# Pooling's differences and the low parts of weights moved between the values, and a queue of loads in program order

## The chip, the cores and the metric

The kernel runs on one core of a Trainium2 chip. The metric is the time of one execution in device microseconds (us); with more cores it would be that of the slowest. The engines are named as in the profile: PE is TensorE (matmuls; PEld its loads of weights), DVE is VectorE, ACT is ScalarE, POOL is GpSimd, and SP is SyncE, which in this kernel only issues DMAs. SP issues its DMAs one after another, and a DMA that has to wait for its data holds back those behind it in the queue.

## The reference, cut to what matters

One block of a transformer with two branches, for one sequence of 1024 positions, a width of 1024 and 16 heads, in float32:

```python
mod = silu(c) @ w_ada + b_ada
shift, scale, gate = split(mod, 3)
h = rms_norm(x, norm_gain) * (1 + scale) + shift
q, k, v, z_a, u, z_b, m_a, m_b = split(h @ w_in, 8)     # each 1024 columns

attn = stick_breaking_attention(q, k, v)                # strictly causal
p_a = (attn * silu(z_a)) @ w_branch_a

# four groups of 256 channels, windows 2, 4, 8, 16
d = trailing_mean(u, window of the group) - u
pooled = (d @ pool_w[group]) * pool_scale
p_b = (pooled * silu(z_b)) @ w_branch_b

merged = sigmoid(m_a) * p_a + sigmoid(m_b) * p_b
return rms_norm(x + gate * (merged @ w_out), final_gain)
```

The change is in how and when d, the parts of the weights in w_in, and the inputs of w_branch_b are prepared. What is computed stays the same.

## The kernel before

**Products.** TensorE multiplies in a rounded form of float32 (`F32R`). To keep the accuracy, each operand is split in a high part (a rounded copy) and a low part (the operand minus its high part), and a product takes three matmuls for each block of 128 rows: high times high, high times low, low times high (`mm3`, lines 152 to 160). A weight tile is 128x1024 (512 KB): eight blocks of 128x128. A tile gives two outputs of 128x512 ("halves" of the sequence), each of 8 x 3 = 24 matmuls, so a tile has 48 matmuls. `split` (lines 103 to 108) makes the two parts, on the engines that its caller names: the high part is a copy (line 116 on VectorE, line 112 on ScalarE), the low part a subtraction (line 107). `load_w` (lines 118 to 121) loads a weight tile on SP's queue and splits it; the raw tiles (tag "raw") and the split ones (tag "whl") have two buffers each.

**Stages in program order.** The input is normed and modulated and turned into h (kept in on-chip memory as high and low part), and the columns of u are computed and stored to DRAM (`u_d`). Then follow four stages that the change touches:

- *The values* (lines 346 to 366): v is computed in 2 x 8 outputs (half of the columns hf, block of positions sb) and stored to `v_d`.
- *The pooling* (lines 370 to 418): for each of four groups (window win), two differences d of 128 channels each are made from u_d on VectorE: the load of u, log2(win) additions for the window sum (line 386), the subtraction (line 390), the tail (lines 392, 393), and the split (lines 116, 107 into dhl). Then for each of the group's two outputs j: a tile of the z_b product (`project`, weights wzb, high part on VectorE, low part on GpSimd), its silu into zs (lines 403, 404), the pool product (two outputs of 6 matmuls, with the small weights phl), the scale (line 416), and the split into gb (lines 417, 418).
- *The product with w_branch_b* (lines 421 to 435): for each of eight tiles j, the weights wb_j are loaded and split (high part on VectorE, low part on GpSimd), a tile wg_j of w_gate is loaded and added up into gacc (VectorE, lines 427, 429), and two outputs pb are computed, copied by ScalarE to sm (line 433) and stored to DRAM by SP (line 434).
- *The gate*, then attention, in which the remaining products of w_in run.

**Low parts made early.** The products during attention use 40 tiles of w_in. For the first 8 (`PLAIN`) the low part is made when they are used. For the other 32 (numbers 8 to 39) it is made ahead by `make_lo` (lines 131 to 140): SP loads the tile (l_raw), ScalarE copies the high part (l_hi), VectorE subtracts it in place, and SP stores the result to `wl_d`. One each is made with the second halves of u (8), then with each output of the values as `LO_V` says (7 in each half hf, 14 in all), and with each tile of the product with w_branch_b as `LO_PB` says (10).

**What sets the order.** A scheduler orders each engine's instructions. It may move an instruction ahead of others of its engine that are not bound to it. An instruction that is given to `tc.keep_in_program_order` is placed behind the instruction that was traced before it on the same engine. Before the change that is used for the first stages only (`pinned`, and `load` at line 204). From the values on, SP's loads are ordered by the scheduler. Tiles come from pools; where a pool is closed, later pools may use its memory.

## Time and profile before

| | us |
|---|---|
| median of 3 runs | 1263.06 |
| range of the 3 runs | 1262.25 to 1266.24 |
| the profiled execution | 1256.96 |
| its span (first to last instruction) | 1255.2 |

The profile is that of one execution. A row of instructions in a timeline gives the start (us from the span's start), the duration, the engine, the line of the kernel, the operation, out<-in by the program's names, the sizes, and in brackets the time that the engine stood idle before it and what it waited for. "SPq" is SP's queue as it issues a DMA. A row by line gives out<-in and the count of instructions, then busy time, mean ns of one, and the idle time just before them with what ended it. A row of DMAs ends with the median us from issue to landing. The granted clock is the share of full speed that the throttle allowed TensorE. In time, the stages that the change touches stand at 125 to 212 us (the values), 212 to 331 (the pooling) and 331 to 419 (the product with w_branch_b).

### The profile page before, as it was taken

The page shows a single profiled execution, that of the slowest core. Times are in us where ns is not written, and L with a number is a line of the kernel's source. Part 1 is how long each engine was busy: PE and PEld are TensorE (multiplying, and loading weights), DVE is VectorE, ACT ScalarE, POOL GpSimd, SP SyncE. Part 2 cuts the span into 40 slices and gives each one's busy share as a digit, 9 for nine tenths or more (in the row PEclk, how much of TensorE's full clock was granted, in tenths as well). Part 3 has the DMA queues.
Part 4 walks back from the last instruction along what each step waited for, and adds up shares of the span by engine and source line. Part 5 has one row for each costly group of instructions (what it writes and reads, how often), then busy time and mean ns, then how long its engine had stood idle before and what let it go on. Part 6 is the DMA issues. An engine that isn't in the chain of part 4 may idle for free.

```text
span 1255.2 us, 16268 instructions
## 1 busy us (share of the span) xinstructions
PE 1225.7 (98%) x5838; PEld 1015.9 (81%) x5838; DVE 808.5 (64%) x1092; ACT 548.9 (44%) x1029; POOL 223.9 (18%) x373
## 2 busy tenths in 40 slices
PE   7999999899999999999999999999999999899997
PEld 6888888678888888888888888888888888788886
DVE  6624442999511168786887878788786864675653
ACT  5554331321110256565556656566665654331101
POOL 1100010111212333322322222122222310000001
PEclk9999999999999999999999999999999999999999
DMA  9539995862344411133323333232233237964522
GB/s 358 212 135 341 321 360 166 293 203 93 116 143 134 160 42 55 65 125 102 106 78 95 117 101 126 90 107 70 92 123 101 92 107 227 374 215 147 192 64 84
DMA packets 72803, 192.46 MB, mean 153 GB/s; under 512 B 7697, under 2 KB 21009, under 8 KB 70802
## 3 DMA queue, kind: packets, MB, share of 16 engines
q1 hardware_dynamic: 61954, 172.28, 40.1%
q10 hardware_dynamic: 10768, 19.14, 4.6%
q8 instruction: 46, 0.75, 0.2%
q14 instruction: 35, 0.29, 0.1%
HBM read 136.86 MB, written 50.34 MB: 149 GB/s over the span
## 4 chain that ended last, share of the span: by engine, by line
PE 77%; issue 9%; DVE 6%; DMA 3%; POOL 2%; ACT 1%; SPq 0%; POOLq 0%; DVEq 0%; ACTq 0%
PE p L92 24%; PE pb L92 7%; PE v L92 7%; PE pa L92 7%; PE o L92 6%; PE wzb L92 5%; PE u L92 4%; PE z L92 4%; PE av L92 4%; PE wt L92 4%; PE ua L92 3%; DVE om L574 1%; PE pool L92 1%; DVE be L575 1%; DMA l_raw<-in_w_in 1%
## 5 line engine op out<-in xcount | busy, mean ns | idle before, releaser
L92 PE MATMUL p<-hT,w 128*128 128x512 f32 x1920 | 534.5, 399 | 0.0
L92 PEld LDWEIGHTS p<-hT,w 128*128 128x128 f32 x1920 | 341.5, 188 | 56.6 <-issue 0.5
L574 DVE TENSOR_TENSOR_SCAN om<-om 128x512 f32<-128x512 f32 (+7 forms) x128 | 175.2, 1368 | 52.3 <-POOL om L572 28.8
L567 ACT ACTIVATE om<-z 128x512 f32<-128x512 f32 (+2 forms) x192 | 94.5, 492 | 103.8 <-PE z L92 101.4
L594 DVE TENSOR_TENSOR wt<-wt,wt 128x512 fp32r<-128x512 f32 (+1 forms) x160 | 100.9, 631 | 46.6 <-ACT wt L593 45.2
L572 POOL TENSOR_SCALAR_AFFINE_SELECT om<-om 128x128 f32<-128x128 f32 x128 | 65.0, 508 | 328.3 <-ACT om L567 302.6
L593 ACT CAST wt<-wt 128x512 fp32r<-128x512 f32 (+1 forms) x160 | 87.3, 546 | 68.6 <-PE wt L92 64.9
L575 DVE TENSOR_TENSOR be<-be,om 128x511 f32<-128x511 f32 (+7 forms) x128 | 99.7, 779 | 10.8 <-DVE om L574 0.5
L92 PE MATMUL pa<-ga,wa 128*128 128x512 f32 x384 | 92.1, 397 | 3.5 <-ACT m_sg L178 3.5
L92 PE MATMUL av<-wt,vv 128*128 128x512 f32 x320 | 94.4, 376 | 0.0
L92 PEld LDWEIGHTS wt<-ident,be 128*128 128x128 f32 x576 | 72.1, 140 | 27.5 <-DVE wt L594 3.2
L568 ACT ACTIVATE be<-z 128x512 f32<-128x512 f32 (+2 forms) x192 | 93.5, 487 | 0.0
L92 PE MATMUL wt<-ident,be 128*128 128x128 f32 x576 | 89.2, 273 | 3.8 <-DVE wt L594 3.8
L92 PE MATMUL wzb<-hT,wzb 128*128 128x512 f32 x384 | 92.3, 396 | 0.0
L92 PE MATMUL o<-wo,mhl 128*128 128x512 f32 (+1 forms) x408 | 89.8, 377 | 0.0
L92 PEld LDWEIGHTS pa<-ga,wa 128*128 128x128 f32 x384 | 73.2, 191 | 20.3 <-ACT m_sg L178 3.9
L92 PE MATMUL pb<-gb,wb 128*128 128x512 f32 x384 | 88.1, 391 | 0.0
L92 PE MATMUL v<-wv,hT 128*128 128x512 f32 x384 | 87.2, 389 | 0.0
L92 PEld LDWEIGHTS wzb<-hT,wzb 128*128 128x128 f32 x384 | 73.1, 191 | 16.3 <-DVE zs L404 0.3
L92 PEld LDWEIGHTS o<-wo,mhl 128*128 128x128 f32 x408 | 73.5, 188 | 14.4
L92 PEld LDWEIGHTS pb<-gb,wb 128*128 128x128 f32 x384 | 72.1, 188 | 15.8
L92 PEld LDWEIGHTS v<-wv,hT 128*128 128x128 f32 x384 | 72.1, 188 | 15.0
(119 smaller groups left out, 1482.9 us busy)
## 6 DMA issues: line engine op xcount, KB each, us to landing
w_raw<-in_w_in SPq DMA_DIRECT2D x40, 512.0 KB, 4.5
l_raw<-in_w_in SPq DMA_DIRECT2D x32, 512.0 KB, 5.6
wl_d<-l_raw SPq DMA_DIRECT2D x32, 512.0 KB, 5.1
w<-wl_d SPq DMA_DIRECT2D x32, 512.0 KB, 3.8
v_d<-vo SPq DMA_DIRECT2D x16, 512.0 KB, 5.2
vv<-v_d SPq DMA_DIRECT2D x8, 1024.0 KB, 5.7
wa_raw<-in_w_branch_a SPq DMA_DIRECT2D x16, 512.0 KB, 4.6
wa<-in_w_mod SPq DMA_DIRECT2D x7, 1024.0 KB, 9.0
```

The lines of the kernel that those rows point to most:

```text
L92: ins = op(*args, **kw)
L567: act.activation(om[:, b0:b0 + n], zp[:, :n], AF.Sigmoid, scale=-0.125)
L568: act.activation(be[:, b0:b0 + n], zp[:, :n], AF.Sigmoid, scale=0.125)
L572: gp.affine_select(out=tl[:, :P], in_=tl[:, :P], pattern=[[1, P]], compare_op=ALU.is_gt, fill=fill, base=0, channel_multiplier=-1)
L574: v.tensor_tensor_scan(om[:, :W], om[:, :W], om[:, :W], 1.0, ALU.mult, ALU.min)
L575: v.tensor_mul(be[:, 1:W], be[:, 1:W], om[:, :W - 1])
L593: act.copy(wt[:, 0, :off], pt[:, :off])
L594: v.tensor_sub(wt[:, 1, :off], pt[:, :off], wt[:, 0, :off].bitcast(F32))
```

## The change

It has four parts.

1. *Differences.* They leave the pooling's loop and become a function, `make_d(j)`. Three are called during the values (`DIFFS`: behind outputs 1, 5 and 10), the other five during the pooling, behind the z_b product of outputs 0, 2, 3, 4 and 5 (`DIFFS_POOL`). They have a pool of their own ("dif") and dhl has four buffers instead of three.
2. *Low parts of w_in.* The values make 3 in each half instead of 7 (6 instead of 14), the pooling makes 10 (`LO_POOL`, none before), the product with w_branch_b makes 8, one a tile (`LO_PB`, 10 before). `make_lo` has two raw buffers instead of three and makes each tile in two halves of 128x512 with one small buffer for l_hi.
3. *The z_b product* splits its weights on ScalarE (high part) and VectorE (low part) instead of VectorE and GpSimd.
4. *The queue.* `issue_paced` issues a DMA on SP and, from the start of the values to the end of the product with w_branch_b, keeps it in program order. It is used by `load_w`, by the load of make_lo, by the load of u and by the store of the values. The store of make_lo, the loads of praw and wg, and the stores of sm are issued as before.

Beside these, zs (and sm) has two buffers instead of three, gacc and bg have memory of their own, and the pool "first" lies on the other side of memory.

```diff
 PLAIN = 8
-LO_V = (1, 1, 1, 1, 1, 1, 1, 0)
-LO_PB = (1, 1, 1, 1, 1, 1, 2, 2)
+LO_V = (0, 1, 0, 1, 0, 1, 0, 0)
+LO_PB = (1, 1, 1, 1, 1, 1, 1, 1)
+
+DIFFS = {1: 0, 5: 1, 10: 2}
+
+DIFFS_POOL = {0: 3, 2: 4, 3: 5, 4: 6, 5: 7}
+LO_POOL = (1, 1, 1, 1, 1, 1, 2, 2)
...
+    paced = [False]
+
+    def issue_paced(dst, src):
+        ins = nc.sync.dma_start(dst, src)
+        if paced[0]:
+            tc.keep_in_program_order(ins)
+
     def load_w(src, name, hi_eng, lo_eng):
         raw = wts.tile([P, KB, P], F32, tag="raw", bufs=2, name=name + "_raw")
-        nc.sync.dma_start(raw.rearrange("p k c -> p (k c)"), src)
+        issue_paced(raw.rearrange("p k c -> p (k c)"), src)
         return split(raw, [P, KB, P], wts, "whl", 2, hi_eng, lo_eng, name)
...
         for _ in range(n):
             i = next(early_lo)
-            raw = pl.tile([P, D], F32, tag="lraw", bufs=3, name=f"l{i}_raw")
-            nc.sync.dma_start(raw, a["w_in"][tiles[i]])
-            hi = pl.tile([P, D], F32R, tag="lhi", bufs=1, name=f"l{i}_hi")
-            act.copy(hi, raw)
-            v.tensor_sub(raw.bitcast(F32R), raw, hi.bitcast(F32))
+            raw = pl.tile([P, D], F32, tag="lraw", bufs=2, name=f"l{i}_raw")
+            issue_paced(raw, a["w_in"][tiles[i]])
+            for hf in range(2):
+                part = raw[:, hf * 512:hf * 512 + 512]
+                hi = pl.tile([P, 512], F32R, tag="lhi", bufs=1, name=f"l{i}_hi{hf}")
+                act.copy(hi, part)
+                v.tensor_sub(part.bitcast(F32R), part, hi.bitcast(F32))
             nc.sync.dma_start(wl_d[i], raw)
 
     def load_parts(i, name):
...
     early = ExitStack()
-    first = early.enter_context(pool("first"))
+    first = early.enter_context(pool("first", side="right"))
...
+    invn = const.tile([P, 16], F32, name="invn")
+    for j in range(16):
+        gp.memset(invn[:, j:j + 1], 1.0 / (16 - j))
+    dhls = {}
+
+    def make_d(j):
+        win = WINDOWS[j // 2]
+        u = dif.tile([P, S + 16], F32, tag="u", bufs=2, name=f"u{j}")
+        v.memset(u[:, S:], 0.0)
+        issue_paced(u[:, :S], u_d[j])
+        cur, n, step = u, S + 16, 1
+        while step < win:
+            nxt = dif.tile([P, S + 16], F32, tag="win", bufs=2, name=f"win{j}_{step}")
+            n -= step
+            v.tensor_add(nxt[:, :n], cur[:, :n], cur[:, step:step + n])
+            cur, step = nxt, 2 * step
+        t0 = S - win + 1
+        d = dif.tile([P, S], F32, tag="win", bufs=2, name=f"d{j}")
+        v.scalar_tensor_tensor(d[:, :t0], cur[:, :t0], 1.0 / win, u[:, :t0], ALU.mult, ALU.subtract)
+        tl = dif.tile([P, 16], F32, tag="tl", bufs=2, name=f"tl{j}")
+        v.tensor_mul(tl[:, :win - 1], cur[:, t0:S], invn[:, 16 - win + 1:])
+        v.tensor_sub(d[:, t0:], tl[:, :win - 1], u[:, t0:S])
+        dhls[j] = split(d, [P, S], dif, "dhl", 4, v, v, f"dhl{j}")
+
+
+    lows = ExitStack()
+    lo = lows.enter_context(pool("lo"))
     with pool("vp") as vp:
...
             use[i](1, ps)
-            make_lo(vp, 1)
+            make_lo(lo, 1)
+        early.close()
+        diffs = ExitStack()
+        dif = diffs.enter_context(pool("dif", side="right"))
+        paced[0] = True
...
                 v.tensor_sub(vo[:, :, 1], pv, vo[:, :, 0].bitcast(F32))
-                nc.sync.dma_start(
+                issue_paced(
                     v_d[4 * hf:4 * hf + 4, :, sb].rearrange("n p c -> p n c"),
                     vo.rearrange("p (n h) i d -> p n (h i d)", h=2).bitcast(F32),
                 )
-                make_lo(vp, LO_V[sb])
-    early.close()
-
-
-    with pool("pb") as pb:
-        invn = pb.tile([P, 16], F32, name="invn")
-        for j in range(16):
-            gp.memset(invn[:, j:j + 1], 1.0 / (16 - j))
+                make_lo(lo, LO_V[sb])
+                if 8 * hf + sb in DIFFS:
+                    make_d(DIFFS[8 * hf + sb])
+
+
+    with ExitStack() as ctx_pb:
+        pb = ctx_pb.enter_context(pool("pb"))
         gb = pb.tile([P, 2, KB, S], F32R, name="gb")
         for g, win in enumerate(WINDOWS):
-            dhl = []
-            for cb in range(2):
-                j = 2 * g + cb
-                u = pb.tile([P, S + 16], F32, tag="u", bufs=2, name=f"u{j}")
...
-                dhl.append(split(d, [P, S], pb, "dhl", 3, v, v, f"dhl{j}"))
+            dhl = [dhls[2 * g], dhls[2 * g + 1]]
             praw = wts.tile([P, 2, 256], F32, tag="raw", bufs=2, name=f"praw{g}")
             nc.sync.dma_start(praw, a["pool_w"][g].rearrange("(k p) d -> p k d", p=P))
             ph, pl_ = split(praw, [P, 2, 256], pb, "phl", 1, v, v, f"phl{g}")
             for ob in range(2):
                 j = 2 * g + ob
-                zs = [pb.tile([P, 512], F32, tag="zs", bufs=3, name=f"zs{j}_{sh}") for sh in range(2)]
+                zs = [pb.tile([P, 512], F32, tag="zs", bufs=2, name=f"zs{j}_{sh}") for sh in range(2)]
 
                 def silu(sh, ps):
                     act.activation(zs[sh], ps, AF.Sigmoid)
                     v.tensor_mul(zs[sh], ps, zs[sh])
 
-                project(CZB + j, f"wzb{j}", silu, v, gp)
+                project(CZB + j, f"wzb{j}", silu, act, v)
+                if j in DIFFS_POOL:
+                    make_d(DIFFS_POOL[j])
                 for sh in range(2):
                     sl = slice(sh * 512, sh * 512 + 512)
                     ps = bank("tr", f"pool{j}_{sh}")
...
                     v.scalar_tensor_tensor(z, ps, psc_v[:, j:j + 1], z, ALU.mult, ALU.mult)
                     act.copy(gb[:, 0, j, sl], z)
                     v.tensor_sub(gb[:, 1, j, sl], z, gb[:, 0, j, sl].bitcast(F32))
-        gacc, bg = (pb.tile([P, S + 16], F32, tag="u", bufs=2, name=n)[:, :D] for n in ("gacc", "bg"))
+                make_lo(lo, LO_POOL[j])
+        diffs.close()
+        late = ctx_pb.enter_context(pool("late", side="right"))
+        gacc, bg = (late.tile([P, D], F32, name=n) for n in ("gacc", "bg"))
         nc.sync.dma_start(bg, a["b_gate"].broadcast_to([P, D]))
         for j in range(KB):
-            sm = [pb.tile([P, 512], F32, tag="zs", bufs=3, name=f"sm{j}_{sh}") for sh in range(2)]
+            sm = [pb.tile([P, 512], F32, tag="zs", bufs=2, name=f"sm{j}_{sh}") for sh in range(2)]
             whl = load_w(a["w_branch_b"][j], f"wb{j}", v, gp)
             wg = wts.tile([P, D], F32, tag="raw", bufs=2, name=f"wg{j}")
             nc.sync.dma_start(wg, a["w_gate"][j * P:(j + 1) * P, :])
...
                 mm3(ps, whl, (gb[:, 0], gb[:, 1]), range(KB), hmov(sh))
                 act.copy(sm[sh], ps)
                 nc.sync.dma_start(pb_d[j][:, sh * 512:sh * 512 + 512], sm[sh])
-            make_lo(pb, LO_PB[j])
+            make_lo(lo, LO_PB[j])
 
         for hf in range(2):
             sl = slice(hf * 512, hf * 512 + 512)
...
         nc.sync.dma_start(g_d, bg[0:1, :])
+    lows.close()
+    paced[0] = False
```

How the change moves instructions is shown at three places. The rows are one engine's instructions in their order, each with its line, operation, out<-in and size; the lines before and after the change differ by some numbers.

The first place is SP's queue from the end of the pooling into the first tiles of the product with w_branch_b. wb1_raw is the second weight tile of that product, wg a tile of w_gate, sm the copied results, sm0_0 those of the first half of tile 0, l32_raw a tile of w_in whose low part is made, wl_d its store. Before:

```order
L120 DMA wb1_raw_2507<-in_w_branch_b 128x1024
L425 DMA wg1_2512<-in_w_gate 128x1024
L120 DMA wb2_raw_2577<-in_w_branch_b 128x1024
L425 DMA wg2_2582<-in_w_gate 128x1024
L120 DMA wb3_raw_2647<-in_w_branch_b 128x1024
L434 DMA pb_d_74<-sm0_0_2435 128x512
L434 DMA pb_d_74<-sm0_1_2436 128x512
L425 DMA wg3_2652<-in_w_gate 128x1024
L434 DMA pb_d_74<-sm1_0_2505 128x512
L120 DMA wb4_raw_2717<-in_w_branch_b 128x1024
```

After:

```order
L457 DMA wg0_2536<-in_w_gate 128x1024
L466 DMA pb_d_74<-sm0_0_2529 128x512
L466 DMA pb_d_74<-sm0_1_2530 128x512
L127 DMA l32_raw_2593<-in_w_in 128x1024
L155 DMA wl_d_76<-l32_raw_2593 128x1024
L127 DMA wb1_raw_2604<-in_w_branch_b 128x1024
L457 DMA wg1_2609<-in_w_gate 128x1024
L466 DMA pb_d_74<-sm1_0_2602 128x512
L466 DMA pb_d_74<-sm1_1_2603 128x512
L127 DMA l33_raw_2666<-in_w_in 128x1024
L155 DMA wl_d_76<-l33_raw_2666 128x1024
```

Before, the load of wb3 stands ahead of the stores of tile 0, and that of wb4 ahead of the second store of tile 1. After, the load of wb1 stands behind both stores of tile 0, the load of l32 and the store of its low part, and the next tile repeats this.

The second place is VectorE's order where the values end and the pooling begins. vo7_1 is the last output of the values, phl0 the small weights of the first group, dhl0 the split difference of the first 128 channels, zs0_0 the first silu. Before:

```order
L361 TENSOR_TENSOR vo7_1_1609<-v7_1_1584,vo7_1_1609 128x8x64
L380 MEMSET u0_1636 128x16
L380 MEMSET u1_1649 128x16
L116 CAST phl0_1664<-praw0_1662 128x512
L107 TENSOR_TENSOR phl0_1664<-praw0_1662,phl0_1664 128x512
L404 TENSOR_TENSOR zs0_0_1667<-wzb0_0_1674,zs0_0_1667 128x512
L386 TENSOR_TENSOR win0_1_1639<-u0_1636 128x1039
L390 SCALAR_TENSOR_TENSOR d0_1641<-win0_1_1639,u0_1636 128x1023
L392 TENSOR_TENSOR tl0_1643<-win0_1_1639,invn_1618 128x1
L393 TENSOR_TENSOR d0_1641<-tl0_1643,u0_1636 128x1
L386 TENSOR_TENSOR win1_1_1652<-u1_1649 128x1039
L116 CAST dhl0_1646<-d0_1641 128x1024
```

After:

```order
L407 TENSOR_TENSOR vo7_1_1668<-v7_1_1643,vo7_1_1668 128x8x64
L154 TENSOR_TENSOR l22_raw_1778<-l22_raw_1778,l22_hi0_1780 128x512
L154 TENSOR_TENSOR l22_raw_1778<-l22_raw_1778,l22_hi1_1783 128x512
L121 CAST phl0_1679<-praw0_1677 128x512
L112 TENSOR_TENSOR phl0_1679<-praw0_1677,phl0_1679 128x512
L431 TENSOR_TENSOR zs0_0_1682<-wzb0_0_1689,zs0_0_1682 128x512
L112 TENSOR_TENSOR wzb1_1791<-wzb1_raw_1789,wzb1_1791 128x1024
L154 TENSOR_TENSOR l23_raw_1868<-l23_raw_1868,l23_hi0_1870 128x512
L431 TENSOR_TENSOR zs0_1_1683<-wzb0_1_1716,zs0_1_1683 128x512
L445 SCALAR_TENSOR_TENSOR zs0_0_1682<-pool0_0_1758,vecs_86,zs0_0_1682 128x512
L154 TENSOR_TENSOR l23_raw_1868<-l23_raw_1868,l23_hi1_1873 128x512
L445 SCALAR_TENSOR_TENSOR zs0_1_1683<-pool0_1_1768,vecs_86,zs0_1_1683 128x512
```

Before, the window sums, the subtractions and the splits of the first differences follow phl0. After, they are gone from here, since the first differences stand among the values; the low parts of w_in (l22, l23) and of the second z_b weights (wzb1) stand in their place.

The third place is VectorE's order where the pooling ends and the product with w_branch_b begins. wb0 and wb1 are the first two weight tiles of that product, gb the split results of the pooling, zs7 the last output's silu and scale. Before:

```order
L416 SCALAR_TENSOR_TENSOR zs6_0_2270<-pool6_0_2331,vecs_86,zs6_0_2270 128x512
L416 SCALAR_TENSOR_TENSOR zs6_1_2271<-pool6_1_2341,vecs_86,zs6_1_2271 128x512
L429 SCALAR_TENSOR_TENSOR gacc_2432<-wg1_2512,csilu_97,gacc_2432 128x1024
L418 TENSOR_TENSOR gb_1635<-zs6_0_2270,gb_1635 128x512
L418 TENSOR_TENSOR gb_1635<-zs6_1_2271,gb_1635 128x512
L404 TENSOR_TENSOR zs7_0_2351<-wzb7_0_2358,zs7_0_2351 128x512
L116 CAST wb1_2509<-wb1_raw_2507 128x1024
L404 TENSOR_TENSOR zs7_1_2352<-wzb7_1_2385,zs7_1_2352 128x512
L416 SCALAR_TENSOR_TENSOR zs7_0_2351<-pool7_0_2412,vecs_86,zs7_0_2351 128x512
L416 SCALAR_TENSOR_TENSOR zs7_1_2352<-pool7_1_2422,vecs_86,zs7_1_2352 128x512
L418 TENSOR_TENSOR gb_1635<-zs7_0_2351,gb_1635 128x512
L418 TENSOR_TENSOR gb_1635<-zs7_1_2352,gb_1635 128x512
```

After:

```order
L431 TENSOR_TENSOR zs7_0_2423<-wzb7_0_2430,zs7_0_2423 128x512
L431 TENSOR_TENSOR zs7_1_2424<-wzb7_1_2457,zs7_1_2424 128x512
L445 SCALAR_TENSOR_TENSOR zs7_0_2423<-pool7_0_2484,vecs_86,zs7_0_2423 128x512
L445 SCALAR_TENSOR_TENSOR zs7_1_2424<-pool7_1_2494,vecs_86,zs7_1_2424 128x512
L447 TENSOR_TENSOR gb_1676<-zs7_0_2423,gb_1676 128x512
L447 TENSOR_TENSOR gb_1676<-zs7_1_2424,gb_1676 128x512
L121 CAST wb0_2533<-wb0_raw_2531 128x1024
L459 TENSOR_SCALAR gacc_2526<-wg0_2536,csilu_97 128x1024
L154 TENSOR_TENSOR l32_raw_2593<-l32_raw_2593,l32_hi0_2595 128x512
L154 TENSOR_TENSOR l32_raw_2593<-l32_raw_2593,l32_hi1_2598 128x512
L121 CAST wb1_2606<-wb1_raw_2604 128x1024
L461 SCALAR_TENSOR_TENSOR gacc_2526<-wg1_2609,csilu_97,gacc_2526 128x1024
```

Before, the high part of wb0 is made ahead of these rows and that of wb1 ahead of the last scale. After, the high part of wb0 follows the pooling's last results, and that of wb1 follows the low part of l32.

14 lines of the change are left out of this document (removed).

## The prediction

> **What bounds the kernel now.** I read the page's busy shares first, then busy time by stage, then the chain of waits of TensorE, then the timeline of the stage that the change touches.
>
> ```profile
> span 1255.2 us, 16268 instructions
> PE 1225.7 (98%) x5838; PEld 1015.9 (81%) x5838; DVE 808.5 (64%) x1092; ACT 548.9 (44%) x1029; POOL 223.9 (18%) x373
> ```
>
> TensorE is busy for 98% of the span, so any change can gain little, and anything that makes TensorE wait is paid in full. The next rows are busy times by stage (start and end, length, PE, PEld, DVE, ACT, POOL, granted clock, DMA share, GB/s): the values, the pooling with its z_b product, and the product with w_branch_b.
>
> ```profile
> 125.00:212.00 87.00, 87.00 (x385) 72.05 (x384) 32.92 (x34) 26.81 (x33) 5.27 (x18) 1.00 0.82 289
> 212.00:331.40 119.40, 112.21 (x482) 90.94 (x481) 109.08 (x142) 29.00 (x42) 21.29 (x8) 0.99 0.54 185
> 331.40:419.30 87.90, 87.90 (x386) 72.12 (x385) 13.91 (x15) 10.61 (x18) 17.56 (x8) 1.00 0.38 129
> ...
> PE pool L92 <- DVE phl L116: 4.0, 1, 4.0
> PE pool L92 <- DVE u L380: 3.1, 1, 3.1
> ...
> 254.00:256.00 2.00, 2.00 (x6) 1.61 (x5) 2.00 (x3) 0.92 (x1) 0.00 (x0) 0.50 0.39 160
> 256.00:258.00 2.00, 2.00 (x7) 1.56 (x7) 2.00 (x4) 0.12 (x1) 0.00 (x0) 0.68 0.58 59
> ```
>
> In the values TensorE never waits and VectorE works 33 us of 87. In the pooling VectorE works 109 us of 119, and TensorE waits for it twice, 4.0 and 3.1 us. After the longer wait the granted clock was 0.50 for 2 us and 0.68 for 2 us: 1.0 + 0.64 = 1.6 us more. That is all there is to gain here: 7.1 + 1.6 = **8.7 us**. In the product with w_branch_b TensorE never waits. Why, the timeline shows:
>
> ```profile
> 331.38 88.06 PE L92 MATMUL pb<-gb,wb 128*128 128x512 f32 x384
> ...
> 342.57 0.59 ACT L433 COPY sm<-pb 128x512 f32<-128x512 f32 x1 [3.94 <-PE pb L92]
> 342.62 0.69 DVE L116 CAST wb<-wb_raw 128x1024 fp32r<-128x1024 f32 x1 [5.60 <-PE pb L92]
> 343.18 0.33 SPq L434 DMA_DIRECT2D pb_d<-sm  x1
> 343.40 2.41 POOL L107 TENSOR_TENSOR wb<-wb_raw,wb 128x1024 fp32r<-128x1024 f32 x1 [11.32 <-DVE wb L116]
> 345.83 0.33 SPq L425 DMA_DIRECT2D wg<-in_w_gate  x1
> 348.06 0.59 ACT L433 COPY sm<-pb 128x512 f32<-128x512 f32 x1 [4.91 <-PE pb L92]
> 348.67 0.32 SPq L434 DMA_DIRECT2D pb_d<-sm  x1
> 349.43 1.28 DVE L429 SCALAR_TENSOR_TENSOR gacc<-wg,csilu,gacc 128x1024 f32<-128x1024 f32 x1 [6.12 <-DMA wg<-in_w_gate]
> 350.75 0.33 SPq L120 DMA_DIRECT2D wb_raw<-in_w_branch_b  x1
> 353.60 0.59 ACT L433 COPY sm<-pb 128x512 f32<-128x512 f32 x1 [4.95 <-PE pb L92]
> ...
> 419.52 0.59 ACT L433 COPY sm<-pb 128x512 f32<-128x512 f32 x1 [4.91 <-PE pb L92]
> ```
>
> A weight tile lasts 353.60 - 342.57 = 11.03 us. The load at 350.75 is that of a tile two ahead; the cast at 342.62 waited for a buffer that TensorE had just left, not for data. Weights are ready a whole tile early.
>
> **The change, part by part.**
>
> *Pooling (gain).* The order puts differences 0 to 3 between the values, so at the start of pooling only phl stands ahead of the first pool product. Four differences cost VectorE 21 us (two of 4.65 and two of 5.9, by the rows below: window sum, subtraction, cast, low part). In the values it then works about 33 + 21 us, less the l tiles that leave, of 87: hidden. In the pooling it loses 21 us, gains 8 low parts of wzb at 1.2 and loses 8 casts at 0.69: about 92 of 112. I take both waits as gone: **-8.7 us**. If the cover fails, up to 7 us stay.
>
> ```profile
> L386 DVE TENSOR_TENSOR win<-u 128x1039 f32<-128x1039 f32 x8 | 9.9, 1234 | 0.3 <-DMA u<-u_d 0.3
> L390 DVE SCALAR_TENSOR_TENSOR d<-win,u 128x1023 f32<-128x1023 f32 x2 | 2.4, 1216 | 0.0
> L417 ACT CAST gb<-zs 128x512 fp32r<-128x512 f32 x16 | 9.9, 621 | 36.0 <-DVE zs L416 32.0 <-DVE u L380 3.9
> L418 DVE TENSOR_TENSOR gb<-zs,gb 128x512 fp32r<-128x512 f32 x16 | 10.8, 680 | 0.1
> L416 DVE SCALAR_TENSOR_TENSOR zs<-pool,vecs,zs 128x512 f32<-128x512 f32 x16 | 11.6, 742 | 2.3 <-PE pool L92 2.2
> ...
> l_raw<-in_w_in SPq DMA_DIRECT2D x32, 512.0 KB, 5.6
> ...
> wb_raw<-in_w_branch_b SPq DMA_DIRECT2D x8, 512.0 KB, 3.4
> ...
> 164.61 0.32 SPq L140 DMA_DIRECT2D wl_d<-l_raw  x1
> 165.03 0.38 SPq L136 DMA_DIRECT2D l_raw<-in_w_in  x1
> ```
>
> *Product with w_branch_b (loss).* Here the order of SP's queue changes. The load of l is pinned behind the two stores of the tile's result, the load of the next wb behind wl_d, the store of l's low part. SP issues one row after the other, and each of these waits for its data. So from the end E of a tile's last matmul everything follows in series, where before it lay a tile ahead:
>
> - copy of the last half 0.08 after E (331.38 + 88.06 = 419.44; copy 419.52); its store 0.61 after the copy's start (348.67 - 348.06); next issue 0.42 later (164.61 to 165.03): load of l at E + 1.11
> - landing as for wb alone, 3.4: E + 4.5
> - two halves, each a cast on ScalarE (0.62) and a low part on VectorE (0.68); the one lhi buffer keeps them in series: 2.6, with hand-overs 2.7: E + 7.2
> - wl_d, then wb 0.42 later: E + 7.65
> - wb's landing: no trace row has this pair alone. Bounds: 3.4 (wb alone) and 5.6 (l among others). I take 4.4, near the alone row, as one 512 KB store runs just ahead: E + 12.0
> - cast 0.69, hand-over 0.09, low part on GpSimd 2.41: E + 15.2. Four matmuls need only the high part and run meanwhile.
> - 44 matmuls at 88.06/384 = 0.229, and 0.16 until the last has drained (0.39 long, 0.23 apart): E + 25.5
>
> A tile takes 25.5 us instead of 11.03: **+14.4 us**. TensorE has stood still some 12 us each time, so the clock will fall as it did at 254. That costs between nothing and 1.6 us, as the four early matmuls and the wait for GpSimd may absorb it; I take 1.0. Tiles 1 to 7: 7 x 15.4 = **+108 us**.
>
> The Trainium skill ("TensorE: Matmul & The Clock Gate", Part 1: The HAM clock gate) says that TensorE falls to half rate after an idle window of about 3.4 us and needs about as long in work to recover. The rows at 254 and 256 agree. By it every restart would cost an estimated 1.7 us, and the total would be 5 us higher.
>
> *First tile of that product.* Before, wb0 was cast while pooling still ran. Now its cast stands behind pooling's last results on VectorE: scale 0.74, cast 0.62, low part 0.68, cast of wb0 0.69, low part 2.41, hand-overs 0.3 = 5.4 us after the last pool product, less four matmuls, 0.9: **+4.5 us**. Between 0, if wb0's row can be served earlier, and 7 with a cold clock.
>
> *At nothing:* smaller lhi (the l casts are hidden where TensorE has other tiles: ScalarE is 44% busy), two zs buffers instead of three, memory sides, invn moved to the start. In the pooling, each odd wzb load is also pinned behind a wl_d. From the start of a tile it takes about 4 us to the load, 3.4 to 5.6 to land, 1.05 + 1.2 for its parts: at most 12, against 48 x 0.229 + 12 x 0.24 = 13.9 us. It fits, with 2 us to spare in the worst case. The loads of u wait for nothing late. In the values v_d's stores stand behind l's, but have three buffers. After the product, the first K and Q tiles load unpinned, and attention is as before.
>
> Sum: 108 + 4.5 - 8.7 = **+104 us**. The profiled execution took 1256.96 us (span 1255.2), the median of the three runs 1263.06, 0.5% more. On the median: 1263 + 104 = **1367 us**.
>
> **The rivals.**
>
> 1. *Not slower: the loads stay ahead.* If l's load and the next wb's were issued at a tile's start, their chain (3.4 + 2.7 + 4.4 + 3.2 = 14 us) could mostly lie beside its 11 us, and with loads a tile further ahead, as the load at 350.75 is, entirely. Then only pooling's gain is left: 1263 - 9 = 1254. It decides itself at one point: whether SP reaches wb's row before the store of the tile under way has its data. For it: the buffers would allow it. Against: the order has store, store, l, wl_d, wb. 3%.
> 2. *Longer: GpSimd is held by VectorE.* In the trace two VectorE operations lasted 3.11 and 3.44 instead of 1.2 while GpSimd formed a low part:
>
> ```profile
> 225.78 2.40 POOL L107 TENSOR_TENSOR wzb<-wzb_raw,wzb 128x1024 fp32r<-128x1024 f32 x1 [35.75 <-DVE wzb L116]
> 226.16 3.11 DVE L107 TENSOR_TENSOR dhl<-d,dhl 128x1024 fp32r<-128x1024 f32 x1
> 239.17 3.44 DVE L390 SCALAR_TENSOR_TENSOR d<-win,u 128x1021 f32<-128x1021 f32 x1
> ```
>
> So the later of two waits for the earlier. gacc (1.28) now follows wb's cast at once if wg has landed by then; if it starts in the 0.09 us before GpSimd does, each tile grows by 1.2: +8.4, 1375. Against it: wg is issued 0.42 behind wb, behind two other transfers. 14%. The Trainium skill ("SBUF — State Buffer", SBUF: two separate sides) says that a VectorE operation with two SBUF inputs and a GpSimd one lock each other out for a whole instruction; the two rows agree.
> 3. *Longer: pooling waits for wzb too.* VectorE's rows now hold wzb's low parts behind differences. If four odd tiles came 5 us late: +20, 1387. 10%.
> 4. *Shorter: half the chain is hidden,* because l's tile is served before TensorE ends: 7 us a tile less, 1318. 5%.
>
> **How the numbers follow.** Forecast 68%, rivals 3, 14, 10 and 5%. Low end: wb at 3.4, no clock loss, no first-tile loss: 7 x 13.4 - 9 = 85, 1348. High end: both landings at 5.6 (+3.4 a tile), clock at 1.6 (+0.6), the lock (+1.2): 7 x 20.6 - 4 = 140, 1403. Range **1346 to 1402**; it leaves out rivals 1 and 4 and corners. A measurement here can tell about 0.3% from no change: faster 3%, the same 1%, slower 96%.
>
> **What would show it.** In the changed profile: TensorE waiting for DVE wb seven times, about 12 us each, in a stage of some 200 us instead of 88; SP rows in the order store, store, l, wl_d, wb; granted clock near half at each restart; no wait of pool for phl or u. Wrong would be: wb's load issued before the store of its tile, tiles of 11 us, or waits of that size in pooling.

## The result and the profile after

| | before | changed |
|---|---|---|
| median | 1263.35 us (4 runs, 1262.25 to 1266.24) | 1376.55 us (4 runs, 1375.46 to 1377.45) |
| profiled execution, its span | 1256.96, 1255.2 us | 1375.46, 1373.4 us |
| ratio to before | | 1.0915, 95% interval 1.0888 to 1.0941 |

The changed kernel is 9.15% slower. The first rows are from its page.

```profile
span 1373.4 us, 16307 instructions
PE 1244.6 (91%) x5838; PEld 1026.3 (75%) x5838; DVE 821.2 (60%) x1124; ACT 561.9 (41%) x1069; POOL 203.0 (15%) x365
```

TensorE's share fell from 98% to 91%. Busy time by stage, with the columns of the prediction's table (start and end, length, PE, PEld, DVE, ACT, POOL, granted clock, DMA share, GB/s), shows where:

```profile
125.00:216.30 91.30, 88.89 (x386) 73.15 (x385) 43.49 (x66) 21.47 (x35) 0.00 (x0) 0.98 0.66 218
216.30:325.30 109.00, 109.00 (x481) 89.82 (x479) 84.03 (x119) 38.59 (x60) 0.00 (x0) 1.00 0.53 181
325.30:539.40 214.10, 111.85 (x389) 83.70 (x390) 40.15 (x35) 19.18 (x32) 21.56 (x9) 0.74 0.28 95
```

The third stage is the product with w_branch_b, with the four gate matmuls that end it. The same stage before:

```profile
331.40:420.60 89.20, 89.20 (x390) 72.70 (x388) 14.18 (x16) 11.69 (x20) 17.56 (x8) 1.00 0.38 127
```

So the values took 91.3 us instead of 87.0 (+4.3), pooling 109.0 instead of 119.4 (-10.4), the product 214.1 instead of 89.2 (+124.9). What follows, 834.0 us (1373.4 - 539.4), was 834.6 before (1255.2 - 420.6). These make +118.2, the difference of the two spans. What TensorE waited for in the changed kernel's stages (total, times, longest):

```profile
PE pb L97 <- DVE wb L121: 97.6, 8, 13.8
...
PE pb L97 <- POOL wb L112: 3.2, 7, 1.3
PE v L97 <- DVE vo L407: 2.4, 1, 2.4
...
PE gate L97 <- DVE gacc L461: 1.4, 1, 1.4
```

The waits of pool for phl and u are gone. In their place stand eight waits for wb. One of them from end to end, in the timeline of the changed kernel (start, duration, engine, line; in brackets the idle time before and what ended it):

```profile
359.39 11.87 PE L97 MATMUL pb<-gb,wb 128*128 128x512 f32 x44 [0.46 <-POOL wb L112]
...
371.30 0.58 ACT L465 COPY sm<-pb 128x512 f32<-128x512 f32 x1 [4.40 <-PE pb L97]
372.28 0.43 SPq L127 DMA_DIRECT2D l_raw<-in_w_in  x1
375.99 0.62 ACT L153 CAST l_hi<-l_raw 128x512 fp32r<-128x512 f32 x1 [4.11 <-DMA l_raw<-in_w_in]
...
378.73 0.32 SPq L155 DMA_DIRECT2D wl_d<-l_raw  x1
379.40 0.33 SPq L127 DMA_DIRECT2D wb_raw<-in_w_branch_b  x1
...
384.01 0.69 DVE L121 CAST wb<-wb_raw 128x1024 fp32r<-128x1024 f32 x1 [5.30 <-DMA wb_raw<-in_w_branch_b]
384.78 2.36 POOL L112 TENSOR_TENSOR wb<-wb_raw,wb 128x1024 fp32r<-128x1024 f32 x1 [25.44 <-DVE wb L121]
384.85 2.04 PE L97 MATMUL pb<-gb,wb 128*128 128x512 f32 x4 [13.59 <-DVE wb L121]
385.23 3.00 DVE L461 SCALAR_TENSOR_TENSOR gacc<-wg,csilu,gacc 128x1024 f32<-128x1024 f32 x1 [0.52 <-DMA wg<-in_w_gate]
...
387.20 11.64 PE L97 MATMUL pb<-gb,wb 128*128 128x512 f32 x44 [0.30 <-POOL wb L112]
```

TensorE ends a tile at 371.26. Only then are the result copied and stored, l loaded, converted and stored, wb loaded, cast and its low part formed, and at 387.20 the next 44 matmuls begin. In between TensorE does four matmuls only, beside GpSimd's low part; nothing else in this chain overlaps its work. The load of wb has no need of l: it only stands behind it.

### The profile page after: what moved, and what is told of

Same layout as the page of the kernel before. It is cut to its first block, busy times and chain, and to the rows that moved or that the text cites. A ratio compares the mean times of both kernels' runs of the same rounds, so it can differ in the third digit from the quotient of the medians.

```text
span 1373.4 us, 16307 instructions
## 1 busy us (share of the span) xinstructions
PE 1244.6 (91%) x5838; PEld 1026.3 (75%) x5838; DVE 821.2 (60%) x1124; ACT 561.9 (41%) x1069; POOL 203.0 (15%) x365
## 4 chain that ended last, share of the span: by engine, by line
PE 66%; DMA 10%; issue 10%; DVE 7%; POOL 4%; ACT 2%; SPq 1%; POOLq 0%; ACTq 0%; DVEq 0%
PE p L97 21%; PE pb L97 7%; PE wzb L97 6%; PE pa L97 6%; PE o L97 6%; DMA l_raw<-in_w_in 4%; PE z L97 3%; PE wt L97 3%; PE av L97 3%; PE v L97 3%; PE ua L97 2%; DMA wb_raw<-in_w_branch_b 2%; PE u L97 2%; PE pool L97 2%; DVE om L608 1%
## 5 line engine op out<-in xcount | busy, mean ns | idle before, releaser
L97 PE MATMUL pb<-gb,wb 128*128 128x512 f32 x384 | 109.2, 447 | 100.9 <-DVE wb L121 97.6
L97 PEld LDWEIGHTS pb<-gb,wb 128*128 128x128 f32 x384 | 82.3, 219 | 127.6 <-issue 98.6
L154 DVE TENSOR_TENSOR l_raw<-l_raw,l_hi 128x512 fp32r<-128x512 f32 x64 | 44.2, 690 | 179.4 <-ACT l_hi L153 178.9
L97 PE MATMUL wt<-ident,be 128*128 128x128 f32 x576 | 89.1, 272 | 4.3 <-DVE wt L628 4.2
L97 PE MATMUL v<-wv,hT 128*128 128x512 f32 x384 | 89.1, 394 | 2.4 <-DVE vo L407 2.4
L97 PE MATMUL wzb<-hT,wzb 128*128 128x512 f32 x384 | 88.4, 389 | 0.0
L112 POOL TENSOR_TENSOR wb<-wb_raw,wb 128x1024 fp32r<-128x1024 f32 x8 | 19.2, 2396 | 451.9 <-DVE wb L121 451.9
```

The lines of the kernel that those rows point to most:

```text
L97: ins = op(*args, **kw)
L112: lo_eng.tensor_tensor(lo, src, hi.bitcast(F32), op=ALU.subtract)
L154: v.tensor_sub(part.bitcast(F32R), part, hi.bitcast(F32))
```

## The experiments

Each kernel was timed beside runs of the kernel before, whose medians lay between 1259.69 and 1263.35 us; so ratios are compared. The stage lengths below are from the profile of one execution each, from first to last matmul of the values, of pooling with its z_b product, and of the product with w_branch_b with the gate; "sum" is that of the three.

| kernel | ratio to before, 95% interval | values | pooling | product | sum |
|---|---|---|---|---|---|
| before | 1 | 87.0 | 119.4 | 89.2 | 295.6 |
| changed | 1.0915 [1.0888, 1.0941] | 91.3 | 109.0 | 214.1 | 414.4 |
| e1 changed, no pins in the product | 0.9931 [0.9905, 0.9957] | 91.7 | 110.0 | 90.2 | 291.9 |
| e2 before, pins in the product alone | 1.0977 [1.0943, 1.1012] | 87.0 | 110.2 | 213.9 | 411.1 |
| e3 changed, wb a tile ahead | 1.0002 [0.9988, 1.0015] | 90.3 | 110.4 | 95.0 | 295.7 |
| e4 changed, the product's l in pooling | 1.0769 [1.0737, 1.0802] | 89.1 | 147.4 | 156.4 | 392.9 |
| e5 changed, no pins | 0.9996 [0.9977, 1.0015] | 93.5 | 112.8 | 88.4 | 294.7 |
| e6 changed, wb's low part on VectorE | 1.0878 [1.0846, 1.0911] | 91.2 | 109.8 | 206.7 | 407.7 |
| e7 e1, four vo buffers | 0.9958 [0.9940, 0.9976] | 91.5 | 108.9 | 90.1 | 290.5 |
| e8 before, z_b split as changed | 1.0000 [0.9980, 1.0020] | 87.1 | 119.6 | 89.3 | 296.0 |
| e9 e1, z_b split as before | 1.0036 [1.0016, 1.0056] | 93.1 | 119.5 | 89.8 | 302.4 |
| e10 changed, pins in pooling alone | 0.9986 [0.9971, 1.0002] | 96.4 | 108.8 | 89.7 | 294.9 |
| e11 e7, second difference earlier | 0.9949 [0.9928, 0.9971] | 90.0 | 108.8 | 89.9 | 288.7 |
| e12 e1, all differences in pooling | 1.0021 [0.9998, 1.0045] | 87.0 | 118.7 | 92.9 | 298.6 |

### Is it the order of SP's queue in the product?

e1 ends the pins ahead of that product, with all else as changed:

```diff
         diffs.close()
+        paced[0] = False
         late = ctx_pb.enter_context(pool("late", side="right"))
```

> The changed kernel, with SP's loads kept in program order only to the end of pooling; the product with w_branch_b loads in the scheduler's order again. Theory (the order of SP's queue in that product makes the loss): its tiles take about 11 us again, no wait of TensorE for wb beyond the first tile; what stays is what the trace shows elsewhere, values +4.3 us, pooling -10.4, first tile 0 to +4, so 1257 to 1261 us, at the widest 1252 to 1264. Rival (the work itself: two l buffers, l_hi in halves, two sm buffers make the stage long whatever the order): still above 1340 us.

Measured: 1252.25 us, 0.9931, at the low edge of the widest bounds and below the likely ones. The product takes 90.2 us. All but 1.0 us of the product's loss goes with this line, and the kernel that is left is faster than before by 0.4 to 1.0%. The rows are TensorE's in e1's product:

```profile
327.13 32.80 PE L97 MATMUL pb<-gb,wb 128*128 128x512 f32 x144
361.42 54.70 PE L97 MATMUL pb<-gb,wb 128*128 128x512 f32 x240 [1.48 <-ACT sm L466]
415.96 1.88 PE L97 MATMUL gate<-gacc,ones 128*128 128x512 f32 x4
```

All 384 matmuls run with one wait of 1.48 us, and none for wb. e2 goes the other way: the kernel before, and only the pins, only there (load_w and the load of make_lo go through issue_paced).

```diff
         nc.sync.dma_start(bg, a["b_gate"].broadcast_to([P, D]))
+        paced[0] = True
...
             make_lo(pb, LO_PB[j])
+        paced[0] = False
```

> The kernel before, with the loads of weights and of l kept in program order in the product with w_branch_b alone; nothing else of the change. Theory: that alone makes the loss. Seven tiles of 28.0 instead of 11.0 us are +119, a second l in tile 6 about 6.5 more, the first tile 0 to +7: 1389 to 1396 us, at the widest 1375 to 1405. Rival (the work itself, or smaller buffers): within 1% of the kernel before, 1251 to 1276.

Measured: 1382.59 us, 1.0977, inside the widest bounds and below the likely ones. The product takes 213.9 us, as in the changed kernel. TensorE's rows for tiles 5 to 7 of e2:

```profile
457.14 2.04 PE L92 MATMUL pb<-gb,wb 128*128 128x512 f32 x4 [13.71 <-DVE wb L116]
...
484.20 2.05 PE L92 MATMUL pb<-gb,wb 128*128 128x512 f32 x4 [13.03 <-DVE wb L116]
486.56 11.65 PE L92 MATMUL pb<-gb,wb 128*128 128x512 f32 x44 [0.31 <-POOL wb L107]
518.74 2.05 PE L92 MATMUL pb<-gb,wb 128*128 128x512 f32 x4 [20.53 <-DVE wb L116]
```

A second l ahead of tile 7's load lengthens its wait from 13.03 to 20.53 us: each l in the chain costs about 7.5 us. What the expectation missed is in the table: e2's pooling also fell, to 110.2 us. In the kernel before, the scheduler lets the ten l tiles of the product run during pooling (L139 x10 in the rows further down); pinned into the product, they no longer take VectorE's time there. That this is what frees pooling fits the rows, but no run tests it alone.

e3 keeps every pin, and only writes the load and split of the next wb ahead of the current tile's matmuls:

```diff
-            whl = load_w(a["w_branch_b"][j], f"wb{j}", v, gp)
+            whl = wbs.pop(j) if j else load_w(a["w_branch_b"][0], "wb0", v, gp)
...
+            if j + 1 < KB:
+                wbs[j + 1] = load_w(a["w_branch_b"][j + 1], f"wb{j + 1}", v, gp)
             for sh in range(2):
```

> The changed kernel with all its pins; only the load and split of wb stand one tile earlier in the program, ahead of the matmuls of the tile before. Theory (what costs is the place in the queue, not that it is pinned): SP reaches wb's row before the stores of the tile under way, so its tiles take 11 us again, and the result is that of the run without pins in the product, 0.990 to 0.998 of the kernel before (1250 to 1260 us). Rival (pinning as such, by taking the scheduler's freedom, costs): still over 1.02.

Measured: 1.0002, just above the expected 0.990 to 0.998, and far from the rival's 1.02. The product takes 95.0 us, 4.8 more than in e1: seven tiles run at full speed, and the difference lies at the first, where the cast of wb0 still stands behind pooling's results on VectorE (2.8 and 0.8 us of waits, and a low clock behind them). So in the seven tiles a pin costs nothing by itself. What costs is the row that it puts ahead.

### How long are the links of the chain?

e4 takes l out of the chain (`LO_PB` all 0) and makes those eight low parts in pooling (`LO_POOL` 2,2,2,2,2,2,3,3).

> The changed kernel, its queue pinned as it is, with the eight low parts of the product with w_branch_b made in pooling instead (18 there, none in the product). Theory (a chain in series, with l's load, its two halves and wl_d as one link): the load of wb can go at about 1.0 instead of 8.1 us after a tile's end, and land in 3.4 to 4.6, so a tile loses 7.1 to 8.3 of its 28.0 us and stays near 20; seven tiles are -50 to -58, 1319 to 1327 us, up to 1345 if the ten more l tiles hold pooling up. Rival (the work on l is the cost, not the order): the tiles go back to 11 us, about 1263. Rival (GpSimd and VectorE hold each other): no change, 1370 or more.

Measured: 1357.37 us, 1.0769, outside my 1319 to 1345. In the product the theory's number came: 156.4 us, 57.7 less, and the waits for wb are 5.9 to 6.5 us instead of 13.1 to 13.8. The miss is in pooling, 147.4 us instead of 109.0. What TensorE waited for in e4:

```profile
PE pb L97 <- DVE wb L121: 43.5, 7, 6.5
PE wzb L97 <- ACT wzb L117: 25.9, 4, 12.9
```

The longest of these waits, in the timeline of e4:

```profile
346.10 0.33 SPq L155 DMA_DIRECT2D wl_d<-l_raw  x1
346.48 0.43 SPq L127 DMA_DIRECT2D wzb_raw<-in_w_in  x1
...
352.29 1.22 PE L97 MATMUL wzb<-hT,wzb 128*128 128x512 f32 x2 [12.87 <-ACT wzb L117]
```

The load of wzb stands behind the store of an l, as that of wb does in the product. With two or three l tiles to a z_b tile this holds TensorE up four times; with the changed kernel's one or two it does not. That is what the prediction's third rival named, "pooling waits for wzb too", but in another way: the rival had wzb's low part late on VectorE, here its load is late on SP. The prediction's line on such loads, "It fits, with 2 us to spare in the worst case", holds for one l ahead of a load and not for more.

e6 asks whether GpSimd and VectorE hold each other up at the cost of the tile: wb's low part goes to VectorE.

```diff
-            whl = load_w(a["w_branch_b"][j], f"wb{j}", v, gp)
+            whl = load_w(a["w_branch_b"][j], f"wb{j}", v, v)
```

> The changed kernel with wb's low part made by VectorE instead of GpSimd. Theory: after the cast the path is four matmuls at a low clock (2.05 us), then a wait of 0.3 for GpSimd; only that wait goes, 0.3 a tile, 1.3 in the first, and the 1.4 us that the gate matmuls wait for gacc behind the held VectorE: -3 to -6 us, 1370 to 1374. Rival (the two engines holding each other is part of each tile's loss): at least 1.2 us a tile, -10 us or more, below 1367.

Measured: 1370.8 us, 1.0878 against 1.0915. The intervals overlap, so the sign rests on the profiles: the span is 1368.4 instead of 1373.4, and a tile lasts 27.13 us (517.98 - 355.20 over six) instead of 27.47 (521.70 - 356.89 over six). That is the 0.3 of a hand-over. GpSimd's 2.36 us lie beside four matmuls at a low clock. The stage is 7.4 us shorter (206.7 instead of 214.1): some 2 us from the tiles, the rest from the first and the last tile. The rival's 1.2 us a tile are not there.

### Where do pooling's gain and the loss in the values come from?

The 4.3 us lost in the values had been costed at nothing. My first theory blamed the pinned queue: a store of v stood behind the loads of praw and wzb, and one copy to vo waited 2.4 us for it. e5 sets `paced[0]` never to True; e10 sets it only around pooling.

> The changed kernel with no load pinned anywhere: the differences in the values, the low parts spread, the z_b split by ScalarE and VectorE stay. Theory: the 4.3 us lost in the values come from the pinned queue (a wl_d and a load wait there, and the stores of v behind them keep vo's buffers), so they go; pooling stays free of its waits, as its differences are early; 0.987 to 0.993 of the kernel before. Rival 1 (the loss in the values comes from VectorE's differences there): 0.993 as in the run without pins in the product. Rival 2 (pooling needs the pins, since l's loads run ahead of those of u and wzb): waits of 7 us or more are back, 0.998 or above.

> The changed kernel with its loads pinned during pooling alone, neither in the values nor in the product with w_branch_b. Theory: the loss in the values goes with the pins there (no wait of v for vo, 87 us again), pooling and product as in the run without pins in the product: 0.987 to 0.992 of the kernel before. Rival (the loss in the values comes from VectorE's differences): 0.993, with the wait of v for vo still 2 us or more.

Measured: 0.9996 and 0.9986, and the values take 93.5 and 96.4 us. **The theory fell**: without pins there the loss is larger (waits of v for vo of 3.9 and 6.6 us in all). In e5 pooling takes 112.8 us, with 3.0 us of waits; the second rival's ratio came, its waits of 7 us did not. e7 gives vo a fourth buffer.

```diff
-                vo = vp.tile([P, 8, 2, HD], F32R, tag="vo", bufs=3, name=f"vo{sb}_{hf}")
+                vo = vp.tile([P, 8, 2, HD], F32R, tag="vo", bufs=4, name=f"vo{sb}_{hf}")
```

> The kernel of the run without pins in the product, with four vo buffers instead of three. If the late stores of v are what holds the values up, ScalarE's 2.4 us of waiting for a store go, and v waits for vo under 1.5 us: 0.989 to 0.991 of the kernel before. If ScalarE's cast of wzb ahead of vo's copy is, the waits stay at 2 us or more: 0.993.

Measured: 0.9958, values 91.5 us, the wait of v still 2.3 us. ScalarE no longer waits for a store, so the store was not what held TensorE. The timeline of e7 shows what does:

```profile
177.81 1.05 ACT L117 CAST wzb<-wzb_raw 128x1024 fp32r<-128x1024 f32 x1 [6.29 <-DMA wzb_raw<-in_w_in]
178.77 0.58 ACT L406 CAST vo<-v 128x512 fp32r<-128x512 f32 x1
178.90 1.23 DVE L112 TENSOR_TENSOR wzb<-wzb_raw,wzb 128x1024 fp32r<-128x1024 f32 x1 [5.73 <-ACT wzb L117]
...
180.26 1.24 DVE L363 TENSOR_TENSOR win<-u 128x1039 f32<-128x1039 f32 x1
181.42 0.68 DVE L407 TENSOR_TENSOR vo<-v,vo 128x512 fp32r<-128x512 f32 x1
...
182.16 2.41 PE L97 MATMUL v<-wv,hT 128*128 128x512 f32 x5 [2.34 <-DVE vo L407]
```

ScalarE's copy of v stands behind the first cast of wzb, which waits 6.29 us for its load. VectorE's low part of v stands behind that of wzb and a window sum. TensorE needs the bank that this low part frees. e12 puts all differences back into pooling:

```diff
-DIFFS = {1: 0, 5: 1, 10: 2}
-DIFFS_POOL = {0: 3, 2: 4, 3: 5, 4: 6, 5: 7}
+DIFFS = {}
+DIFFS_POOL = {0: 2, 1: 3, 2: 4, 3: 5, 4: 6, 5: 7}
...
+        make_d(0)
+        make_d(1)
         for g, win in enumerate(WINDOWS):
```

> The kernel of the run without pins in the product, with all eight differences back in pooling (two ahead of its first product, six behind the z_b products 0 to 5). Theory (the differences made during the values are what takes pooling's waits away): waits of pool for VectorE of 4 to 8 us are back, and the clock loss behind them, 0.998 to 1.004 of the kernel before; the values keep their loss if it comes from the queue and the z_b split, and lose it if it comes from the differences. Rival (the order of the loads in pooling is what helps): pooling has no such wait, 0.993 or less.

Measured: 1.0021. The values run their 384 matmuls in 87.0 us without a wait, and pooling takes 118.7 us, with 5.1 us of waits of pool. So the differences made during the values cost 4.7 us there (91.7 in e1), and free 8.7 us in pooling (110.0). e11 takes e7 and makes the second difference behind output 3 instead of 5, away from the first wzb (`DIFFS = {1: 0, 3: 1, 10: 2}`).

> The kernel of the run with four vo buffers, with the second difference made behind output 3 of the values instead of 5. There its window sum (1.24 us, after 0.13 of waiting for its u) stands on VectorE between the low part of the first wzb and that of vo, while TensorE waits 2.3 us for that vo. Theory (that place of a difference on VectorE is what is left of the loss in the values): v waits 0.5 to 1.2 us for vo, the values take 88 to 90 us instead of 91.5, the whole 0.992 to 0.995 of the kernel before. Rival (the cast of wzb that waits for its load is all of it): still 2 us or more of waiting and about 91 us, 0.996.

Measured: 0.9949, values 90.0 us, one wait of 1.71 us. The wait lies between the two expectations. The 1.5 us gained in the values are not all wait (0.6 us less): behind e7's wait the granted clock is 0.50 from 182.5 to 185.5, behind e11's it stays at 1.00. So the window sum is likely part of the loss and the cast of wzb that waits for its load another; this rests on one execution each, and how they divide stays open. e1, e7 and e11 cannot be told apart by their ratios; each beats both kernels.

Does pooling gain from the differences alone? e8 gives the kernel before the new split of z_b (`project(CZB + j, f"wzb{j}", silu, act, v)`), and e9 gives e1 the old one (`v, gp`).

> The kernel before with the weights of z_b split by ScalarE and VectorE instead of VectorE and GpSimd, nothing else. Theory (pooling's waits come from the differences that stand ahead of its first products on VectorE): VectorE gets 4 us more work there, and the waits of pool stay at 7 us or grow; 0.998 to 1.005 of the kernel before. Rival (the split is what takes the waits away): 0.992 to 0.994.

> The kernel of the run without pins in the product, with the weights of z_b split by VectorE and GpSimd as before the change. Theory of the 4 us lost in the values (on ScalarE the copies of v stand behind the first cast of wzb, which waits 6.4 us for its load): v waits for vo less than 1.5 us, the values take 87 to 89 us, pooling stays free of waits; 0.988 to 0.991 of the kernel before. Rival (the stores of v behind the loads of praw and wzb in SP's queue hold vo's buffers): as without this edit, 0.993, with 2 us or more of waits of v for vo.

Measured: 1.0000 and 1.0036. The split alone changes nothing (119.6 us), as expected, though the waits of pool were 4.5 us and not 7. But with the differences moved and the split left on GpSimd, pooling takes 119.5 us too, against my expectation. So with the l tiles made in pooling both are needed; e2, without them, needs neither.

The values of e9 went against it as well: 93.1 us instead of 87 to 89, with 3.8 us of waits of v for vo. Rows of e9 show why:

```profile
179.09 0.69 DVE L121 CAST wzb<-wzb_raw 128x1024 fp32r<-128x1024 f32 x1 [4.64 <-DMA wzb_raw<-in_w_in]
...
181.55 1.82 DVE L363 TENSOR_TENSOR win<-u 128x1039 f32<-128x1039 f32 x1 [1.77 <-DMA u<-u_d]
...
183.30 0.68 DVE L407 TENSOR_TENSOR vo<-v,vo 128x512 fp32r<-128x512 f32 x1
...
184.03 34.58 PE L97 MATMUL v<-wv,hT 128*128 128x512 f32 x144 [3.27 <-DVE vo L407]
```

Taken off ScalarE, the cast that waits for wzb's load stands on VectorE, and a window sum that waits for its own load behind it, both ahead of vo's low part. The block has only moved.

Groups of VectorE by line in pooling (count, then busy us, mean ns) show what GpSimd does to VectorE; first the kernel before, then e8:

```profile
L107 DVE TENSOR_TENSOR dhl<-d,dhl 128x1024 fp32r<-128x1024 f32 x8 | 15.3, 1908 | 0.0
L139 DVE TENSOR_TENSOR l_raw<-l_raw,l_hi 128x1024 fp32r<-128x1024 f32 x10 | 12.1, 1211 | 0.1
```

```profile
L107 DVE TENSOR_TENSOR dhl<-d,dhl 128x1024 fp32r<-128x1024 f32 x8 | 9.8, 1220 | 0.0
```

The first subtraction takes 1908 ns in the mean where GpSimd forms eight low parts in the same stretch, and 1220 ns where it forms two. The mean hides two sizes: in the kernel before, three of the eight start while GpSimd forms a low part and take 3.04 to 3.11 us, the other five take 1.21 or 1.22. The subtractions of the l tiles stay at 1211 ns. That such holds make e9's pooling slow fits its rows (four first additions of a window sum at 1781 ns instead of 1234), but is argued and not shown.

## Why the prediction was right, point by point

Its time, 1367 us, is 9.55 us below the 1376.55 measured, and that lies inside 1346 to 1402. (The two ends as worked out there are 1348 and 1403.)

**The product: right in mechanism, short in size.** The term was +108 for seven tiles and +4.5 for the first, 112.5; the stage measured +124.9. The links for the tile shown above, from the end of the matmuls (371.26):

| step | predicted | measured |
|---|---|---|
| load of l issued | 1.11 | 1.02 |
| l's landing | 3.4 | 3.71 |
| conversions until wl_d | 2.7 | 2.74 |
| wl_d until wb | 0.42 | 0.67 |
| wb's landing | 4.4 | 4.61 |
| cast, hand-overs, low part, until the 44 matmuls | 3.2 | 3.19 |
| 44 matmuls, with the lower clock | 11.2 | 11.64 |
| tile | 26.5 | 27.58 |

No link was missing. Tiles were 27.47 us in the mean, about 1.0 more than the forecast. The first tile measured +7.0 (325.30 to 331.00 + 12.38 is 18.08 us, against 11.03): its bound of 7 "with a cold clock" was the truth, the 4.5 that I chose left the clock out. The last tile was another 3.8 us longer, since TensorE's gate matmuls moved into it (at 1.06 us each instead of 0.59, behind 1.4 us of waiting for gacc); before, they took 1.15 us behind the last tile. No term stood for that.

**Pooling: right.** -8.7 was the term, -10.4 the measurement. Both waits went (7.1). The other 3.3 are more than the 1.6 put down for the clock: behind the second wait 30 matmuls took 8.55 us (253.36 to 261.91) instead of 30 x 0.229 = 6.9, so the clock had cost about 1.7; where the last 1.6 lay stays open. The cause as given was incomplete: I argued from VectorE's 21 us less of differences; e9 shows that taking the z_b split off GpSimd is needed as well, and e2 that pooling is as short with the l tiles held back and neither of the two.

**The values: wrong by 4.3 us.** "In the values it then works about 33 + 21 us, less the l tiles that leave, of 87: hidden." VectorE had the time (43.49 us busy of 91.30), but not in the right order: an engine that takes its instructions in order had a wait for a load ahead of an instruction that TensorE needed. Of the 4.3 us, 2.4 are the wait; most of the rest is the clock behind it: 144 matmuls took 34.51 us instead of 32.8 at the pace of the 240 before them (54.56 us). The line on v_d's stores, "but have three buffers", was aimed at the wrong place: a copy to vo did wait 2.40 us for such a store, but TensorE's wait ended with VectorE's low part (181.21 + 0.68 is 181.89), and with a fourth buffer it is as long (e7).

**The rivals.** "The loads stay ahead" came true neither in the order nor on the chip; e1 is that case, 1252.25 us against its 1254. "GpSimd is held by VectorE" came out reversed: gacc starts 0.45 us after GpSimd, and it is VectorE that is stretched, 3.00 us instead of 1.28, with no cost to the tile except at the gate. So its 1375 us, nearer to the measurement than the forecast, is near by luck. "Pooling waits for wzb too" did not happen; e4 shows that one more l a tile brings it about, through SP's queue. "Half the chain is hidden": nothing was.

The sum was made against the profiled execution. Its difference is 118.2 us, that of the medians 113.2; the execution profiled before lay 6.4 us under its median, that after only 1.1. So the sum of 104 us was 14 us short against the profile it was made from (12.4 in the product, 4.3 in the values, less 1.7 in pooling and 0.6 after it). That the forecast missed the median by 9.55 us only is in part luck.

## What to carry to other kernels

A queue kept in program order turns the way the code is written into a schedule: a load written behind a store waits for that store's data, needed or not, so write it where it should be issued (a tile ahead), as e3 did with every pin in place. When an edit moves work into an engine's idle time, ask not how much idle time there is, but which instruction stands behind the moved one and what the moved one itself waits for. Price such a chain link by link from rows that already stand in the trace: seven links priced so were each within 0.5 us.

## What the runs showed of the hardware

Where TensorE's granted clock falls in these three stages of the changed kernel, it does so 2.4 to 5.2 us after its work stops, and in the values and tiles 1 to 6 it comes back 3.4 to 5.9 us after work starts again. The windows behind the matmuls that end at 371.26, with the columns as above:

```profile
371.00:376.00 5.00, 0.26 (x2) 0.00 (x0) 0.00 (x0) 0.60 (x2) 0.00 (x0) 1.00 0.47 157
376.00:378.00 2.00, 0.00 (x0) 0.00 (x0) 0.69 (x1) 1.22 (x2) 0.00 (x0) 0.62 0.00 0
378.00:384.00 6.00, 0.00 (x0) 0.00 (x0) 0.69 (x1) 0.00 (x0) 0.00 (x0) 0.50 0.75 253
```

```profile
384.00:388.00 4.00, 2.84 (x6) 1.86 (x7) 3.47 (x2) 0.00 (x0) 2.36 (x1) 0.50 0.04 16
388.00:390.00 2.00, 2.00 (x6) 1.52 (x6) 0.23 (x1) 0.00 (x0) 0.00 (x0) 0.50 0.00 0
390.00:392.00 2.00, 2.00 (x10) 1.66 (x9) 0.00 (x0) 0.00 (x0) 0.00 (x0) 0.97 0.00 0
```

The clock is full until 376, mixed in 376 to 378 and 0.50 after (a mean of 0.62 puts its fall near 376.5, 5.2 us after the stop); work starts again at 384.85 and the clock is full from about 390. A much shorter wait lowers it too. In the values the matmuls stop at 179.53 and start again at 181.94:

```profile
179.50:181.50 2.00, 0.03 (x1) 0.00 (x0) 1.84 (x3) 0.00 (x0) 0.00 (x0) 1.00 0.84 299
182.00:185.00 3.00, 3.00 (x7) 2.42 (x8) 2.92 (x6) 0.10 (x1) 0.00 (x0) 0.50 0.78 227
185.50:187.00 1.50, 1.50 (x8) 1.24 (x7) 0.37 (x1) 0.00 (x0) 0.00 (x0) 1.00 0.60 230
```

So 2.4 us after the stop, as work returns, the clock is at half. In e1 TensorE waits longer at the same place, 2.73 us (180.88 to 183.62), and the clock stays at 1.00 from 181 to 191: the length of the wait alone does not decide. The Trainium skill ("TensorE: Matmul & The Clock Gate", Part 1: The HAM clock gate) sets the clock by windows of about 3.4 us that run freely; a wait that must cover one whole window lowers the clock somewhere between 3.4 and 6.8 us after its start (an estimate from that page). The 5.2 us behind 371.26 lie within that; the 2.4 us of the values do not, so here a wait need not cover a whole window, and the measurement decides.

The restarts cost the 44 matmuls of tiles 1 to 6 some 1.3 us each (11.32 to 11.87 instead of 44 x 0.229 + 0.16 = 10.24); the prediction's estimate by that page was 1.7. A shorter wait was not cheaper in clock: in e4, where TensorE stood still for about 6 us, 44 matmuls took 10.89 to 11.98 us.

An operation on VectorE such as gacc's, or the subtractions into dhl, that starts while GpSimd forms a low part ends about 1.1 us after GpSimd does, nearly its own length, as if it began only then (gacc: 385.23 + 3.00 is 388.23, 1.1 us past GpSimd's 387.14), while GpSimd keeps its 2.36 us. It does not hold for all: in the kernel before, at 278.55, the silu's multiply, which reads a result of TensorE, keeps its 0.68 us inside a low part that GpSimd forms from 277.58 to 280.91.
